# Half-size weight transfers, and matrix-vector work between half units, in a float32 decoder trunk

## The chip, the cores and the metric

The kernel runs on one core of a Trainium2 chip. The metric is the device time of one execution in microseconds, median of several runs. The engines: PE (TensorE) multiplies matrices, ACT (ScalarE) and DVE (VectorE) do elementwise work, POOL (GpSimd) does little here, and SP (SyncE) issues nearly all transfers from device memory. Each engine works through its own instructions in order and waits on semaphores for the others.

## The reference

A trunk of two layers on one sequence of 256 tokens, width 2048. All weights are float32. Each of the four sub-layers is normalised and modulated by vectors made from a conditioning vector `c`:

```python
cond = jax.nn.silu(c)
for l in range(DEPTH):                                   # DEPTH = 2
    mod = cond @ ada_w[l] + ada_b[l]                     # ada_w[l]: 2048 x 12288
    sh1, sc1, g1, sh2, sc2, g2 = jnp.split(mod, 6, axis=-1)
    h = modulate(rmsnorm(x, norm_mix_g[l]), sh1, sc1)    # h * (1 + sc) + sh
    y = mixer_ab(h, ...) if l % 2 == 0 else mixer_c(h, ...)
    x = x + g1 * y
    h = modulate(rmsnorm(x, norm_ffn_g[l]), sh2, sc2)
    x = x + g2 * swiglu(h, ffn_w1[l], ffn_w3[l], ffn_w2[l])   # width 5632
return rmsnorm(x, final_g)
```

`mixer_ab` has one input projection 2048 x 4096 (`ab_w_in`), a causal convolution of width 31 (`a_conv_w`) with a layer norm on one half, spatial gating on the other, and an output projection 2048 x 2048. `mixer_c` is a pooling mixer with four 512 x 512 matrices.

## The kernel before

All weights, 537 MB, stream once from device memory through a ring of buffers named `raw`, the pool `rawp`: six buffers of 1 MB (`RAW = 6`). SP issues each load as soon as a buffer of the ring is free again.

**Products.** The tokens lie in two blocks of 128 (`NB = 2`, index b). Activations are kept transposed and in two parts, `ah` and `al` (the float32 value rounded to PE's fast format, and the rest); q = 0 to 3 numbers groups of 512 input channels, and `act[q][b]` holds the two parts of one group and block. A *unit* (`unit`, `load`) is a 512 x 512 tile of weights. It is split in two halves of 256 rows: ACT casts the half to `hi` (L165) and DVE subtracts to get `lo` (L166), in rings of four (`HL = 4`). Then PE does 12 products a half: for both blocks and two k-tiles hi·ah (L206) and hi·al (L207), and lo·ah (L212) behind them. `block` does the same for several units.

**Matrix-vector work.** The vectors of `mod` come as `cond @ ada_w`, generators that make one step at each `next`. `mod_cols` (L365 on) makes 512 columns of one vector: four steps, each with one load of 512 x 512 and four matmuls with a 32-column broadcast of `cond` (L382, tile `ps_ada`); the fourth also copies the sum to `rows` on ACT (L399); the rest, run by `close`, adds the four strips with four small matmuls (`ps_col`, L412), and DVE adds the bias and writes columns of `gs` (scale) or `sh` (shift). `mod` (L308) makes a whole vector as a row, with wide loads of 128 x 2048 (L304). `weighed` (L343, L354) does the sums on DVE instead. Such work is called a *matvec* below, as one matmul of it.

**The stage of `started`.** It runs the first three column groups of layer 0's input projection while the scale and shift columns of the next group are still being made, since `h` of group q needs only group q's columns. For each q it first writes the instructions that scale the activations of q (`scaled`: `h` at L506, half of it on ACT and half on DVE, then the cast to `ah`, L495), then units u = 0, 1, 2. A matvec generator pair (scale, shift) for q+1 goes beside them: after u0 the scale's four steps, after u1 the shift's four steps; each is closed in the middle of the next unit. The third unit's sums are called `mt`. Before the stage, SP loads the scale matrix for q = 0 (4 units), then x (two blocks of 1 MB, L984), then the shift matrix; ACT squares x (L465, `junk`), x is normalised and transposed (`tp`, L486), copied to `xT`. Small parameters are loaded on ACT's queue at the start, among them `a_conv_w` (31 rows, L621) into tile `prm`. PE transposes the parameters (`tp`, L634 and L639) into `wcT` and `cw` behind q = 0, in `params`.

**Order of the work.** The program is written as these loops; a scheduler then places instructions of independent work in each engine's order by their expected readiness. DMA completions use eight semaphores in rotation over both queues (SP and ACT) in the order of the program, and a transfer waits until the one before it on its semaphore is done.

Of the kernel before, what the change touches and what calls it, by code (L numbers as in the profile page):

```python
# [8 lines left out]
F32 = mybir.dt.float32  # L9
F32R = mybir.dt.float32r  # L10
AF = mybir.ActivationFunctionType
ALU = mybir.AluOpType
PSUM = bass.MemoryType.PSUM

P = 128
D = 2048
KT = D // P
# [3 lines left out]
DH = D // 2  # L21
# [2 lines left out]
PADA = CW - 1  # L24
PADC = 16
EPS = 1e-6
RAW, HL = 6, 4
RATES = 1.56, 0.71, 0.5, 1.0, 1.0
PE2 = False
PE3 = True  # L30
# [6 lines left out]
class Trunk:  # L37
# [119 lines left out]
        return t  # L157


    def split(self, raw, h):  # L160
        nc = self.nc
        hi = self.hip.tile([P, 2, 512], F32R, name="hi", tag="hi")
        lo = self.lop.tile([P, 2, 512], F32R, name="lo", tag="lo")
        part = raw[:, 2 * h : 2 * h + 2, :]
        nc.scalar.copy(hi, part)  # L165
        nc.vector.tensor_tensor(lo, part, hi.bitcast(F32), op=ALU.subtract)  # L166
        for _ in range(FILL):
            self.filler()
        return hi, lo
# [8 lines left out]
                self.fill.pop(0)  # L178

    def load(self, w, row0, col0):  # L180
        raw = self.rawp.tile([P, 4, 512], F32, name="raw", tag="raw")
        self.nc.sync.dma_start(
            out=raw,
            in_=w[row0 : row0 + 512, col0 : col0 + 512].rearrange("(k p) n -> p k n", p=P),
        )
        return raw

    def unit(self, w, row0, col0, act, ps, first, last, mid=None):


        raw = self.load(w, row0, col0)
        for h in range(2):
            if h == 1 and mid is not None:
                mid()
            hi, lo = self.split(raw, h)
            for b in range(NB):
                self.products(hi, lo, h, act, b, ps, first)
            for b in range(NB):
                self.products_lo(hi, lo, h, act, b, ps, last)
        self.after_unit()  # L200
# [15 lines left out]
    def block(self, cells, hooks={}):  # L216


        parts = []
        for w, row0, col0, *_ in cells:  # L220
            raw = self.load(w, row0, col0)
            parts.append([self.split(raw, h) for h in range(2)])
        for b in range(NB):
            for u, (_, _, _, act, ps, first, last) in enumerate(cells):
                for h in range(2):
                    for f in hooks.get((b, 2 * u + h), ()):
                        f()
                    hi, lo = parts[u][h]
                    self.products(hi, lo, h, act, b, ps, first)
                    self.products_lo(hi, lo, h, act, b, ps, last)  # L230
        for _ in cells:
            self.after_unit()
# [62 lines left out]
    def mod(self, l, v, on_pe, then):  # L295


        nc = self.nc
        w = self.i["ada_w"][l]
        if on_pe:  # L300
            ps = self.adap.tile([P, 512], F32, name="ps_ada", tag="ada")
            for k in range(KT):
                raw = self.rawp.tile([P, 4, 512], F32, name="raw", tag="raw")
                nc.sync.dma_start(  # L304
                    out=raw.rearrange("p a n -> p (a n)"), in_=w[k * P : (k + 1) * P, v * D : (v + 1) * D]
                )
                for j in range(4):
                    nc.tensor.matmul(  # L308
                        ps[32 * j : 32 * j + 32, :], self.cond[:, k : k + 1].to_broadcast([P, 32]),
                        raw[:, j, :], start=k == 0, stop=k == KT - 1, skip_group_check=True,  # L310
                    )
                if k < KT - 1:
                    yield
        else:
            ps = None
            for hh in range(2):
                acc = self.accp.tile([P, DH], F32, name="acc", tag="acc")
                for _ in self.weighed(acc, l, v * D + DH * hh):
                    yield
                if ps is None:  # L320
                    ps = self.adap.tile([P, 512], F32, name="ps_ada", tag="ada")
                for j in range(2):
                    o = 32 * (2 * hh + j)
                    nc.tensor.matmul(
                        ps[o : o + 32, :], self.ones[:, :32], acc[:, 512 * j : 512 * j + 512],
                        start=True, stop=True, skip_group_check=True,
                    )
                if hh == 0:
                    yield
        rows = self.wk.tile([P, 512], F32, name="rows", tag="rows", bufs=1)  # L330
        nc.vector.tensor_tensor(  # L331
            rows, ps, self.load_rows(self.i["ada_b"][l, v * D : (v + 1) * D]), op=ALU.add
        )
        then(rows)
        yield

    def weighed(self, acc, l, col0):

        nc = self.nc
        for u in range(KT // 2):  # L340
            raw = self.rawp.tile([P, 4, 512], F32, name="raw", tag="raw")
            r2 = raw.rearrange("p (k a) n -> p k (a n)", k=2)
            nc.sync.dma_start(  # L343
                out=r2,
                in_=self.i["ada_w"][l, 2 * u * P : 2 * (u + 1) * P, col0 : col0 + DH].rearrange(
                    "(k p) n -> p k n", p=P
                ),
            )
            for j in range(2):
                k = 2 * u + j  # L350
                if k == 0:
                    nc.vector.tensor_scalar(acc, r2[:, j, :], self.cond[:, 0:1], None, op0=ALU.mult)
                else:
                    nc.vector.scalar_tensor_tensor(  # L354
                        acc, r2[:, j, :], self.cond[:, k : k + 1], acc, op0=ALU.mult, op1=ALU.add
                    )
            if u < KT // 2 - 1:
                yield
# [10 lines left out]
    def mod_cols(self, l, v, q, on_pe, dst, gname=None):  # L369


        nc = self.nc
        if on_pe:
            acc = self.adap.tile([P, 512], F32, name="ps_ada", tag="ada")
        else:
            acc = self.accp.tile([P, 2, 512], F32, name="accq", tag="acc")
        for u in range(4):
            raw = self.load(self.i["ada_w"][l], 512 * u, v * D + 512 * q)
            for j in range(4):
                k = 4 * u + j  # L380
                if on_pe:
                    nc.tensor.matmul(  # L382
                        acc[32 * j : 32 * j + 32, :], self.cond[:, k : k + 1].to_broadcast([P, 32]), raw[:, j, :],
                        start=u == 0, stop=u == 3, skip_group_check=True,
                    )
                elif k < 2:
                    nc.vector.tensor_scalar(
                        acc[:, k, :], raw[:, j, :], self.cond[:, k : k + 1], None, op0=ALU.mult
                    )
                else:  # L390
                    nc.vector.scalar_tensor_tensor(
                        acc[:, k % 2, :], raw[:, j, :], self.cond[:, k : k + 1], acc[:, k % 2, :],
                        op0=ALU.mult, op1=ALU.add,
                    )
            if u < 3:
                yield
        if on_pe:
            rows = self.wk.tile([P, 512], F32, name="rows", tag="rows", bufs=1)
            nc.scalar.copy(rows, acc)  # L399
            parts = [(rows, self.pick)]  # L400
        else:
            parts = [(acc[:, n, :], self.ones[:, :1]) for n in range(2)]
        yield
        self.put_cols(parts, 4, l, v, 4 * q, dst, gname)
        yield
# [125 lines left out]
    def close(self, g):  # L531
        if g in self.bg:
            for _ in g:
                pass
            self.bg.remove(g)

    def started(self, e, w_cols, rate, then=None):

        self.rate = 0.0
        ps = [self.banks(), self.banks()]
        ps.append([self.tpp.tile([P, 512], F32, name=f"mt{b}", tag="tp") for b in range(NB)])
        for g in e.parts[0]:
            self.close(g)
        for q in range(4):
            e.act[q] = [self.scaled(e.act[q][b], q, b, e.gs, e.sh) for b in range(NB)]
            nxt = e.parts[q + 1] if q < 3 else ()
            for u, (w, col0) in enumerate(w_cols):
                mid = (lambda g=nxt[u - 1]: self.close(g)) if nxt and u > 0 else None  # L550
                self.unit(w, 512 * q, col0, e.act[q], ps[u], q == 0, q == 3, mid)
                if nxt and u < 2:
                    self.advance(nxt[u], 4)
            if q == 0 and then is not None:
                then()
        self.rate = rate
        return ps
# [514 lines left out]
```

## Time and profile before

| | |
|---|---|
| median of 3 runs | 2023.05 us (2021.81, 2026.48, 2023.05) |
| profiled execution | 2021.9 us, span of the records 2020.2 us |
| mean granted PE clock | 0.991 |
| PE busy | 1968.7 us, 97% |
| DVE, ACT busy | 1342.7 us, 839.1 us |
| moved from device memory | 536.68 MB, mean 267 GB/s |

The records of the span are one execution. A line such as `PE mt L206 <- ACT hi L165` names a wait: PE's line 206, for tile `mt`, waited for ACT's line 165, tile `hi`. A matmul of float32 data such as a matvec makes two records, so x16 matvecs of the program are x32 in a timeline. The clock that is granted to PE is 1.00 or 0.50.

### The profile page before, as it was taken

What the parts mean: (1) busy time and instruction counts of PE and PEld (TensorE: products, weight loads), DVE (VectorE), ACT (ScalarE), POOL (GpSimd) and SP (SyncE); (2) the same over time, 40 slices, a digit from 0 to 9 for tenths busy, and PEclk for the clock granted to TensorE, in tenths of its full rate; (3) what the DMA queues carried; (4) which work ended last, traced back from release to release, by engine and by line L of the source; (5) the groups of instructions that cost most, each with busy time, mean ns of one, the idle gap of its engine ahead of it and who ended that gap; (6) DMA issues with size and microseconds to landing.
All of it is one profiled execution on the core that took longest, in us unless ns stands there. A gap on an engine that the chain in (4) does not pass through costs nothing.

```text
span 2020.2 us, 23411 instructions
## 1 busy us (share of the span) xinstructions
PE 1968.7 (97%) x9136; PEld 1541.6 (76%) x9136; DVE 1342.7 (66%) x1596; ACT 839.1 (42%) x1029; POOL 34.1 (2%) x91
## 2 busy tenths in 40 slices
PE   5989999999999999999999999999999999999998
PEld 2557676767887888887878887788788888888886
DVE  2337998656777887777877788777555444554455
ACT  3233243445444343443344436544433444334443
POOL 0000000000000000000120000000000000000000
PEclk9989999999999999999999999999999999999999
DMA  9897988786888898888988877788655555555551
GB/s 348 301 371 283 353 300 308 264 300 219 294 316 301 323 336 316 302 304 316 343 293 305 297 274 267 292 296 309 226 187 188 188 188 188 187 188 190 190 189 57
DMA packets 240160, 540.30 MB, mean 267 GB/s; under 512 B 8394, under 2 KB 9722, under 8 KB 237617
## 3 DMA queue, kind: packets, MB, share of 16 engines
q1 hardware_dynamic: 238296, 536.95, 74.8%
q10 hardware_dynamic: 1752, 1.86, 0.3%
q8 instruction: 71, 1.16, 0.2%
q14 instruction: 41, 0.33, 0.0%
HBM read 536.68 MB, written 2.10 MB: 267 GB/s over the span
## 4 chain that ended last, share of the span: by engine, by line
PE 96%; DVE 1%; ACT 1%; DMA 1%; issue 0%; POOL 0%; ACTq 0%; POOLq 0%; SPq 0%
PE mm L206 28%; PE mm L207 27%; PE mm L212 27%; PE ps_ada L382 3%; PE ps_col L412 1%; PE mt L206 1%; PE mt L207 1%; PE mt L212 1%; PE tp L589 1%; PE ps_ada L308 1%; DMA st_b<-in_ada_b_dram 1%; PE tp L486 1%; PE tp L836 1%; DMA raw<-in_ada_w_dram 0%; PE ps_bc L436 0%
## 5 line engine op out<-in xcount | busy, mean ns | idle before, releaser
L166 DVE TENSOR_TENSOR lo<-raw,hi 128x1024 fp32r<-128x1024 f32 x632 | 767.6, 1222 | 434.8 <-ACT hi L165 426.7
L165 ACT CAST hi<-raw 128x1024 fp32r<-128x1024 f32 x632 | 661.5, 1054 | 894.8 <-PE mm L207 825.4
L206 PE MATMUL mm<-hi,ah 128*128 128x512 f32 x1568 | 618.1, 394 | 5.4 <-ACT hi L165 3.4
L207 PE MATMUL mm<-hi,al 128*128 128x512 f32 x1568 | 612.8, 391 | 0.0
L212 PE MATMUL mm<-lo,ah 128*128 128x512 f32 x1568 | 421.9, 390 | 0.0
L206 PEld LDWEIGHTS mm<-hi,ah 128*128 128x128 f32 x1568 | 295.4, 188 | 83.4 <-ACT hi L165 10.2
L207 PEld LDWEIGHTS mm<-hi,al 128*128 128x128 f32 x1568 | 295.5, 188 | 61.3 <-DVE lo L166 1.2
L212 PEld LDWEIGHTS mm<-lo,ah 128*128 128x128 f32 x1568 | 294.8, 188 | 61.7
L206 PE MATMUL mm<-hi,hh 128*128 128x512 f32 x704 | 279.9, 398 | 0.0
L207 PE MATMUL mm<-hi,hl 128*128 128x512 f32 x704 | 277.9, 395 | 0.0
L354 DVE SCALAR_TENSOR_TENSOR acc<-raw,cond,acc 128x1024 f32<-128x1024 f32 x180 | 230.4, 1280 | 19.6 <-DMA raw<-in_ada_w_dram 18.1
L212 PE MATMUL mm<-lo,hh 128*128 128x512 f32 x704 | 194.7, 395 | 0.0
L206 PEld LDWEIGHTS mm<-hi,hh 128*128 128x128 f32 x704 | 132.3, 188 | 34.3 <-ACT hi L165 1.7
L212 PEld LDWEIGHTS mm<-lo,hh 128*128 128x128 f32 x704 | 132.2, 188 | 32.0
L207 PEld LDWEIGHTS mm<-hi,hl 128*128 128x128 f32 x704 | 132.3, 188 | 30.9
L674 DVE SCALAR_TENSOR_TENSOR co<-aT,cw,co 128x256 f32<-128x256 f32 x240 | 97.9, 477 | 0.0
L382 PE MATMUL ps_ada<-raw,cond 128*32 128x512 f32 x576 | 86.8, 627 | 0.8 <-DVE rows L331 0.8
L597 DVE TENSOR_TENSOR gy<-mm,gate 128x512 f32<-128x512 f32 x72 | 47.1, 685 | 39.9 <-PE mm L212 39.7
L206 PE MATMUL mm<-hi,mh 128*128 128x512 f32 x160 | 64.5, 404 | 0.9 <-ACT mh L495 0.9
L207 PE MATMUL mm<-hi,ml 128*128 128x512 f32 x160 | 63.0, 395 | 0.0
L399 ACT COPY rows<-ps_ada 128x512 f32<-128x512 f32 x18 | 10.5, 585 | 109.7 <-PE ps_ada L382 109.6
L598 DVE TENSOR_TENSOR x<-x,gy 128x512 f32<-128x512 f32 x72 | 47.2, 685 | 0.2
(167 smaller groups left out, 992.7 us busy)
## 6 DMA issues: line engine op xcount, KB each, us to landing
raw<-in_ffn_w_dram SPq DMA_DIRECT2D x264, 1024.0 KB, 5.2
raw<-in_ada_w_dram SPq DMA_DIRECT2D x192, 1024.0 KB, 6.9
raw<-in_ab_w_in_dram SPq DMA_DIRECT2D x32, 1024.0 KB, 7.5
raw<-in_ab_w_out_dram SPq DMA_DIRECT2D x16, 1024.0 KB, 4.9
raw<-in_pool_w_dram SPq DMA_DIRECT2D x4, 1024.0 KB, 5.5
x<-in_x_dram SPq DMA_DIRECT2D x2, 1024.0 KB, 14.2
gate<-in_final_g_dram SPq DMA_DIRECT2D x1, 1024.0 KB
out_dram<-x SPq DMA_DIRECT2D x2, 512.0 KB, 3.7
```

The costliest lines, as they stand in the source:

```text
L165: nc.scalar.copy(hi, part)
L166: nc.vector.tensor_tensor(lo, part, hi.bitcast(F32), op=ALU.subtract)
L206: nc.tensor.matmul(ps[b], act[b][0][:, kk, :], hi[:, k, :], start=first and kk == 0, stop=False)
L207: nc.tensor.matmul(ps[b], act[b][1][:, kk, :], hi[:, k, :], start=False, stop=False)
L212: self.nc.tensor.matmul(ps[b], act[b][0][:, kk, :], lo[:, k, :], start=False, stop=last and kk == 3)
L308: nc.tensor.matmul(ps[32 * j : 32 * j + 32, :], self.cond[:, k : k + 1].to_broadcast([P, 32]), raw[:, j, :], start=k == 0, stop=k == KT - ...
L354: nc.vector.scalar_tensor_tensor(acc, r2[:, j, :], self.cond[:, k : k + 1], acc, op0=ALU.mult, op1=ALU.add)
L382: nc.tensor.matmul(acc[32 * j : 32 * j + 32, :], self.cond[:, k : k + 1].to_broadcast([P, 32]), raw[:, j, :], start=u == 0, stop=u == 3, s ...
L412: nc.tensor.matmul(ps[:, a : a + 1], src[:, P * a : P * a + P], one, start=u == 0, stop=u == len(parts) - 1,)
L597: nc.vector.tensor_tensor(t, ps, g[:, 512 * q : 512 * q + 512], op=ALU.mult)
L598: nc.vector.tensor_tensor(xs, xs, t, op=ALU.add)
L674: nc.vector.scalar_tensor_tensor(co[:, k, :], src, cw[:, k, j : j + 1], co[:, k, :], op0=ALU.mult, op1=ALU.add,)
```

## The change

Every load of weights and matvec matrices is halved: the ring has twelve buffers of 512 KB, `load` brings 256 rows x 512 columns, and the new `load_wide` 128 rows x 1024 columns. `unit` and `block` load two halves and split each. In `started` the two generators of q+1 are advanced in six slots, in the middle and at the end of each unit, by `between`: the scale takes two steps in the middle of u0 and two after u0, is closed in the middle of u1, where the shift takes two steps; the shift takes two more after u1, and is closed in the middle of u2.

```diff
-RAW, HL = 6, 4
+RAW, HL = 12, 4
...
-    def split(self, raw, h):
+    def split(self, raw):
...
-        part = raw[:, 2 * h : 2 * h + 2, :]
-        nc.scalar.copy(hi, part)
-        nc.vector.tensor_tensor(lo, part, hi.bitcast(F32), op=ALU.subtract)
+        nc.scalar.copy(hi, raw)
+        nc.vector.tensor_tensor(lo, raw, hi.bitcast(F32), op=ALU.subtract)
...
     def load(self, w, row0, col0):
-        raw = self.rawp.tile([P, 4, 512], F32, name="raw", tag="raw")
+        raw = self.rawp.tile([P, 2, 512], F32, name="raw", tag="raw")
...
-            in_=w[row0 : row0 + 512, col0 : col0 + 512].rearrange("(k p) n -> p k n", p=P),
+            in_=w[row0 : row0 + 256, col0 : col0 + 512].rearrange("(k p) n -> p k n", p=P),
...
+    def load_wide(self, w, row0, col0):
+        raw = self.rawp.tile([P, 2, 512], F32, name="raw", tag="raw")
+        wide = raw.rearrange("p a n -> p (a n)")
+        self.nc.sync.dma_start(out=wide, in_=w[row0 : row0 + P, col0 : col0 + DH])
+        return raw, wide
...
     def unit(self, w, row0, col0, act, ps, first, last, mid=None):
-        raw = self.load(w, row0, col0)
+        raws = [self.load(w, row0 + 256 * h, col0) for h in range(2)]
         for h in range(2):
             if h == 1 and mid is not None:
                 mid()
-            hi, lo = self.split(raw, h)
+            hi, lo = self.split(raws[h])
...
     def weighed(self, acc, l, col0):
...
-            for j in range(2):
-                k = 2 * u + j
+            for k in (2 * u, 2 * u + 1):
+                raw = self.load_wide(self.i["ada_w"][l], k * P, col0)[1]
...
     def mod_cols(self, l, v, q, on_pe, dst, gname=None):
-            raw = self.load(self.i["ada_w"][l], 512 * u, v * D + 512 * q)
+            raws = [self.load(self.i["ada_w"][l], 512 * u + 256 * h, v * D + 512 * q) for h in range(2)]
...
+    def between(self, gens, slot):
+
+        if gens and slot in (2, 4):
+            self.close(gens[slot // 2 - 1])
+        if gens and slot < 4:
+            self.advance(gens[slot // 2], 2)
+
     def started(self, e, w_cols, rate, then=None):
...
-                mid = (lambda g=nxt[u - 1]: self.close(g)) if nxt and u > 0 else None
-                self.unit(w, 512 * q, col0, e.act[q], ps[u], q == 0, q == 3, mid)
-                if nxt and u < 2:
-                    self.advance(nxt[u], 4)
+                self.unit(
+                    w, 512 * q, col0, e.act[q], ps[u], q == 0, q == 3, lambda: self.between(nxt, 2 * u)
+                )
+                self.between(nxt, 2 * u + 1)
```

The rows below are each engine's instructions in the order in which it works through them, before and after (the line numbers of the two versions differ by a few).

PE, q = 0, from the last products of u1 to the first of u2 (`mm_314` and `mm_315` are the sums of u1 for the two blocks, `mt_316` that of u2). Before:

```order
L212 MATMUL mm_314<-lo,ah_349 128x512 x2
L212 MATMUL mm_315<-lo,ah_358 128x512 x2
L382 MATMUL ps_ada<-raw,cond 32x512 x16
L412 MATMUL ps_col<-pick,rows 128x1 x4
L634 MATMUL tp<-ident,prm 128x128 x4
L639 MATMUL tp<-ident,prm 128x31 x4
L634 MATMUL tp<-ident,prm 128x128 x4
L206 MATMUL mt_316<-hi,ah_349 128x512
```

After the change (`mm_324`, `mm_325` and `mt_326` are these sums):

```order
L214 MATMUL mm_325<-hi,al_375 128x512
L378 MATMUL ps_ada<-raw,cond 32x512 x2
L219 MATMUL mm_324<-lo,ah_365 128x512 x2
L219 MATMUL mm_325<-lo,ah_374 128x512
L378 MATMUL ps_ada<-raw,cond 32x512 x2
L219 MATMUL mm_325<-lo,ah_374 128x512
L378 MATMUL ps_ada<-raw,cond 32x512 x8
L408 MATMUL ps_col<-pick,rows 128x1 x4
L637 MATMUL tp<-ident,prm 128x128 x4
L642 MATMUL tp<-ident,prm 128x31 x4
L213 MATMUL mt_326<-hi,ah_365 128x512
```

The one group of sixteen shift matvecs has become five, of 2, 2, 2, 2 and 8 (the first two stand earlier, in the second half of u1); one set of four 128x128 transposes no longer stands ahead of u2. The same happens in q = 1 and q = 2, without the transposes; in the whole stage 7 groups become 25.

ACT, at the start of u2 in q = 1 (`h_769`, `h_778` and `ah_774` belong to the activations of q = 2, blocks 0 and 1; the two `hi` to u2 of q = 1). Before:

```order
L399 COPY rows<-ps_ada 128x512 [waits PE_49,Activation_49]
L506 ACTIVATE h_769<-xT_252,sh_141,gs_140 128x128 [waits DVE_49]
L506 ACTIVATE h_769<-xT_252,sh_141,gs_140 128x128
L506 ACTIVATE h_778<-xT_294,sh_141,gs_140 128x128
L495 CAST ah_774<-h_769 128x512 [waits DVE_49,Activation_49]
L165 CAST hi<-raw 128x1024 [waits DMAHW4_49]
L165 CAST hi<-raw 128x1024
```

After the change (the tiles are now `h_829`, `ah_834` and `h_838`):

```order
L395 COPY rows<-ps_ada 128x512 [waits PE_49,Activation_49]
L502 ACTIVATE h_829<-xT_262,sh_141,gs_140 128x128 [waits DVE_49]
L502 ACTIVATE h_829<-xT_262,sh_141,gs_140 128x128
L164 CAST hi<-raw 128x1024 [waits DMAHW1_49]
L491 CAST ah_834<-h_829 128x512 [waits DVE_49,Activation_49]
L164 CAST hi<-raw 128x1024 [waits DMAHW2_49]
L502 ACTIVATE h_838<-xT_304,sh_141,gs_140 128x128 x2
```

The first `hi` of u2 now stands ahead of `ah` and of block 1's `h`, and each `hi` waits for a transfer of its own.

SP, at the start of the program. `DMAHW3_49` is the completion semaphore on which the load of `a_conv_w` stands before the change, `DMAHW4_49` the one on which it stands after it. Before:

```order
L182 DMA raw<-in_ada_w_dram 128x4x512
L182 DMA raw<-in_ada_w_dram 128x4x512 [waits DMAHW0_49]
L182 DMA raw<-in_ada_w_dram 128x4x512 [waits DMAHW4_49]
L182 DMA raw<-in_ada_w_dram 128x4x512 [waits DMAHW7_49]
L182 DMA raw<-in_ada_w_dram 128x4x512 [waits DMAHW1_49]
L984 DMA x_190<-in_x_dram 128x2048 [waits DMAHW2_49]
L984 DMA x_201<-in_x_dram 128x2048 [waits DMAHW3_49]
```

After the change:

```order
L182 DMA raw<-in_ada_w_dram 128x2x512 [waits DMAHW5_49]
L182 DMA raw<-in_ada_w_dram 128x2x512 [waits DMAHW6_49]
L182 DMA raw<-in_ada_w_dram 128x2x512 [waits DMAHW7_49]
L182 DMA raw<-in_ada_w_dram 128x2x512 [waits DMAHW2_49]
L182 DMA raw<-in_ada_w_dram 128x2x512 [waits DMAHW4_49]
L182 DMA raw<-in_ada_w_dram 128x2x512 [waits DMAHW5_49]
L182 DMA raw<-in_ada_w_dram 128x2x512 [waits DMAHW6_49]
L987 DMA x_200<-in_x_dram 128x2048 [waits DMAHW7_49]
L987 DMA x_211<-in_x_dram 128x2048 [waits DMAHW0_49]
```

Before, only the second block of x stood behind the load of `a_conv_w`; after the change the eighth half of `ada_w` does, with two more halves and both blocks of x behind it on the queue.

More of the change, by code (lines that the diff above doesn't have):

```diff
@@ L220, in block @@
         for w, row0, col0, *_ in cells:
-            raw = self.load(w, row0, col0)
-            parts.append([self.split(raw, h) for h in range(2)])
+            raws = [self.load(w, row0 + 256 * h, col0) for h in range(2)]
+            parts.append([self.split(r) for r in raws])
         for b in range(NB):
@@ L302, in mod @@
             for k in range(KT):
[L303 to L306, printed above, removed]
+                raws = [self.load_wide(w, k * P, v * D + DH * h)[0] for h in range(2)]
                 for j in range(4):
@@ L309, in mod @@
                         ps[32 * j : 32 * j + 32, :], self.cond[:, k : k + 1].to_broadcast([P, 32]),
-                        raw[:, j, :], start=k == 0, stop=k == KT - 1, skip_group_check=True,
+                        raws[j // 2][:, j % 2, :], start=k == 0, stop=k == KT - 1, skip_group_check=True,
                     )
@@ L340, in weighed @@
         for u in range(KT // 2):
[L341 to L348, printed above, removed]
-            for j in range(2):
-                k = 2 * u + j
+            for k in (2 * u, 2 * u + 1):
+                raw = self.load_wide(self.i["ada_w"][l], k * P, col0)[1]
                 if k == 0:
-                    nc.vector.tensor_scalar(acc, r2[:, j, :], self.cond[:, 0:1], None, op0=ALU.mult)
+                    nc.vector.tensor_scalar(acc, raw, self.cond[:, 0:1], None, op0=ALU.mult)
                 else:
                     nc.vector.scalar_tensor_tensor(
-                        acc, r2[:, j, :], self.cond[:, k : k + 1], acc, op0=ALU.mult, op1=ALU.add
+                        acc, raw, self.cond[:, k : k + 1], acc, op0=ALU.mult, op1=ALU.add
                     )
@@ L382, in mod_cols @@
                     nc.tensor.matmul(
-                        acc[32 * j : 32 * j + 32, :], self.cond[:, k : k + 1].to_broadcast([P, 32]), raw[:, j, :],
+                        acc[32 * j : 32 * j + 32, :], self.cond[:, k : k + 1].to_broadcast([P, 32]), raws[j // 2][:, j % 2, :],
                         start=u == 0, stop=u == 3, skip_group_check=True,
@@ L387, in mod_cols @@
                     nc.vector.tensor_scalar(
-                        acc[:, k, :], raw[:, j, :], self.cond[:, k : k + 1], None, op0=ALU.mult
+                        acc[:, k, :], raws[j // 2][:, j % 2, :], self.cond[:, k : k + 1], None, op0=ALU.mult
                     )
@@ L391, in mod_cols @@
                     nc.vector.scalar_tensor_tensor(
-                        acc[:, k % 2, :], raw[:, j, :], self.cond[:, k : k + 1], acc[:, k % 2, :],
+                        acc[:, k % 2, :], raws[j // 2][:, j % 2, :], self.cond[:, k : k + 1], acc[:, k % 2, :],
                         op0=ALU.mult, op1=ALU.add,
```

## The prediction

> **What bounds the kernel now.** I read the page's busy times first, then tables of windows for the stages, then the waits of PE (TensorE) inside one stage, and last short stretches of the timeline. A windows row gives start:end, its length, then busy us and instructions of PE, weight load, DVE, ACT and POOL, the granted PE clock, the DMA share and GB/s; a wait row gives total us, times and longest.
>
> ```profile
> PE 1968.7 (97%) x9136; PEld 1541.6 (76%) x9136; DVE 1342.7 (66%) x1596; ACT 839.1 (42%) x1029; POOL 34.1 (2%) x91
> 48.00:152.00 104.00, 91.17 (x483) 59.48 (x484) 36.27 (x55) 35.28 (x51) 0.00 (x0) 0.92 0.88 336
> 152.00:440.00 288.00, 287.10 (x1452) 199.46 (x1452) 227.63 (x398) 108.00 (x149) 3.66 (x4) 1.00 0.84 304
> 466.00:2010.00 1544.00, 1542.37 (x6968) 1256.22 (x6967) 1049.40 (x1075) 659.89 (x760) 22.98 (x66) 1.00 0.72 254
> PE mt L206 <- ACT hi L165: 6.0, 2, 3.0
> PE ps_col L412 <- ACT rows L399: 4.7, 6, 1.1
> PE mm L206 <- ACT hi L165: 3.4, 1, 3.4
> PE tp L639 <- DVE wcT L635: 0.8, 1, 0.8
> PE mm L206 <- ACT ah L495: 2.0, 1, 2.0
> 90.00:92.00 2.00, 2.00 (x13) 1.36 (x14) 0.00 (x0) 0.58 (x1) 0.00 (x0) 1.00 0.00 0
> 120.00:122.00 2.00, 2.00 (x11) 1.65 (x10) 0.00 (x0) 0.00 (x0) 0.00 (x0) 1.00 1.05 408
> 124.00:126.00 2.00, 2.00 (x17) 0.95 (x19) 0.00 (x0) 0.00 (x0) 0.00 (x0) 1.00 0.00 0
> SPq L182 <- DVE lo L166: 977.9, 232, 14.3
> ```
>
> PE bounds the kernel. From 152 us on it is busy 287.10 of 288 and 1542.37 of 1544 us, so nothing that only moves transfers can gain there. The stage of `started`, 48 to 152 us, is different: 91 of 104 us busy at a mean clock of 0.92. The first four wait rows, all of that window, are for ACT and DVE work on data that has already landed; none is for a transfer. The fifth is at the start of the first feed-forward part, near 458 us. The DMA engines reach 408 GB/s and then stand still at 90 and at 124 us while PE is fully busy: the ring is full, and SP waits for splits (978 us of waiting for `lo`).
>
> **The change, part by part.** The profiled execution took 2021.9 us; the median of the runs is 2023.05, 1.15 more. I sum against the first and then add the 1.15.
>
> *The ring and the halves.* Twelve buffers of 512 KB hold the same 6 MB, and the bytes stand in the same order on SP's queue. The number of splits, products and DVE matvec steps stays, with the same tiles. What is added is 508 DMA issues and their semaphores on SP. An issue took 0.41 us (the row of `cs`, below), so 208 us more in all; SP's 978 us of waiting for `lo` cover it. If that cover were gone, the loads would come late, which is a rival below. A half buffer comes free after its own `lo`, so loads may start a little earlier; that gain goes into a DMA idle time that PE never waits for. I take 0; below by the ends of the two DMA rivals.
>
> *The matvecs between half units.* In the stage of `started` PE's matvecs stood in 7 groups and stand in 25 after the change, by the order of instructions: 18 more interruptions of the products. The price of one is read where the kernel already does this (start us, us, what):
>
> ```profile
> 179.73 1.07 PE L212 MATMUL mm<-lo,ah 128*128 128x512 f32 x4
> 180.73 1.92 PE L308 MATMUL ps_ada<-raw,cond 128*32 128x512 f32 x16
> 182.59 0.50 PE L206 MATMUL mm<-hi,ah 128*128 128x512 f32 x1
> 257.95 1.07 PE L212 MATMUL mm<-lo,ah 128*128 128x512 f32 x4
> 258.95 1.06 PE L382 MATMUL ps_ada<-raw,cond 128*32 128x512 f32 x8
> 259.94 0.50 PE L206 MATMUL mm<-hi,ah 128*128 128x512 f32 x1
> 67.87 3.64 PE L382 MATMUL ps_ada<-raw,cond 128*32 128x512 f32 x32
> ```
>
> Four products at the stride of 0.227 us (1.07 less the last one's tail) take 0.91. From the first of the four to the next product there are 2.86 us at 179.73 and 1.99 at 257.95, so 1.95 and 1.08 belong to 8 and to 4 matvecs (a matvec is two records). The difference, 0.87 for 4, is 0.217 each; what is left, 0.21 to 0.23, is fixed for each group. A group of 16 by this is 3.66 us, against the 3.64 shown. So 18 x 0.23 = **+4.1 us**, all on PE's path. No group of two is seen in this trace: the ends are 0 (its fixed part overlaps the product behind it) and twice, 8.2. I take the middle value, since three group sizes agree on it.
>
> *The start of u2.* After the last group of q, PE does `ps_col` and then waits for `hi`.
>
> ```profile
> 107.31 1.05 PE L412 MATMUL ps_col<-pick,rows 128*128 128x1 f32 x8 [0.76 <-ACT rows L399]
> 111.36 0.80 PE L206 MATMUL mt<-hi,ah 128*128 128x512 f32 x1 [3.00 <-ACT hi L165]
> 108.59 1.26 ACT L506 ACTIVATE h<-xT,sh,gs 128x128 f32<-128x128 f32 x3 [1.34 <-DVE sh L418]
> 109.76 0.60 ACT L495 CAST ah<-h 128x512 fp32r<-128x512 f32 x1
> 110.27 1.99 ACT L165 CAST hi<-raw 128x1024 fp32r<-128x1024 f32 x2
> 72.30:75.72 3.42, 1.99 (x16) 1.69 (x16) 1.88 (x6) 2.08 (x6) 0.00 (x0) 1.00 1.05 408
> 106.44:109.85 3.41, 1.16 (x12) 0.97 (x8) 1.27 (x5) 1.84 (x5) 0.00 (x0) 1.00 1.05 410
> 109.85:113.26 3.41, 1.90 (x5) 1.53 (x6) 2.61 (x3) 3.38 (x7) 0.00 (x0) 0.50 1.05 407
> 113.26:116.68 3.42, 3.42 (x10) 2.68 (x9) 3.38 (x4) 1.93 (x3) 0.00 (x0) 0.50 1.06 411
> 137.16:140.57 3.41, 2.65 (x27) 0.77 (x19) 0.00 (x0) 0.58 (x1) 0.00 (x0) 1.00 1.05 409
> 140.57:143.98 3.41, 0.80 (x8) 0.72 (x7) 1.85 (x6) 2.37 (x5) 0.00 (x0) 1.00 1.05 408
> 143.98:147.40 3.42, 3.02 (x7) 2.44 (x8) 3.17 (x5) 3.39 (x6) 0.00 (x0) 0.50 1.05 408
> ```
>
> u2 works on the old activations, but ACT prepares part of the next ones first. The new order puts the first `hi` before the third `h` and the `ah` cast: (109.76 - 108.59)/3 + (110.27 - 109.76) = 0.39 + 0.51 = 0.90 us earlier, in q1 and in q2. PE's gap goes from 3.0 to 2.1. The `h` and `ah` behind it are due only when u2 ends, some five us later, so nobody waits for them.
>
> The clock must be counted too. In the rows it halves in stretches of 3.41 us, and always right behind a stretch in which PE was busy 1.99 us or less; behind 2.65 it stayed full. I slid the pattern (0.76 idle, 1.05 `ps_col`, the gap) over such a grid in small steps, with a half stretch behind each one under 2.4 us busy. The loss of one place, idle and half clock together, averages 5.8 us for a gap of 3.0 (4.9 to 6.7) and 4.75 for 2.1 (4.0 to 5.7). The two places of this profile lost 6.4 and 5.3 by the same count, just the mean. So 2 x -1.05 = **-2.1 us**; ends -3.7 (both at 4.0) and -0.3 (both at 5.7).
>
> The Trainium skill, "TensorE: Matmul & The Clock Gate", Part 1, says that the clock falls to half after at least one idle window of about 3.4 us, and its rule for kernels asks for no PE gap over about 3 us. The 3.41 us raster agrees. The trigger does not: the window at 106.44 had 1.16 us of work and the one at 72.30 had 1.99, and each was followed by half clock. By the rule read strictly the new gap of 2.1 would leave the clock alone, which is the second rival.
>
> In q0 the same place holds transposes of parameters as well. Four of them move behind the first products of u2, and with them part of a wait of 0.8 for `wcT`: **-0.4 us**. Ends: 0, and -1.9 if the stretch at 72.30 then has over 2.65 us of work and the 1.5 us lost to the half clock behind it go too.
>
> *The start.* Completion semaphores of transfers are used in rotation, and the new count shifts them.
>
> ```profile
> 0.80 0.41 SPq L74 DMA_DIRECT2D cs<-in_c_dram  x1
> SPq L984 <- DMA prm<-in_a_conv_w_dram: 8.0, 1, 8.0
> 12.65 8.73 SPq L984 DMA_DIRECT2D x<-in_x_dram  x2
> x<-in_x_dram SPq DMA_DIRECT2D x2, 1024.0 KB, 14.2
> raw<-in_ab_w_out_dram SPq DMA_DIRECT2D x16, 1024.0 KB, 4.9
> 28.04 0.63 ACT L465 ACTIVATE junk<-x 128x512 bf16<-128x512 f32 x1
> ```
>
> Now SP stands 8.0 us behind `conv_w`, from 13.0 to 21.0, with 5 MB of matrix and x0 already issued; x0 lands at 12.65 + 14.2 = 26.9, and ACT squares it at 28.0. In the new order the eighth half is what waits for `conv_w`, and behind it on SP's queue stand two more halves, x0 and x1. From 21.0: 1.5 MB and x0 at 408 GB/s (1 MB in 2.57 us) take 6.4, plus 2.3 from issue to first data (4.9 - 2.57), so x0 lands at 29.7 and the squares begin 1.6 late. The chain from there over the transposes to u0 has PE and ACT work only: **+1.6 us**. Ends: -1.0 if `conv_w` itself lands early because less stands before it, +3 if SP waits for more of the small transfers.
>
> *The rest.* The start of the first feed-forward part shuffles a few instructions around its wait of 2.0 for `ah`; I take 0, ends -2 and +2. The 4 KB rows of `load_wide` instead of 8 KB ones lie in a stretch where PE is 100% busy: 0.
>
> Sum: 4.1 - 2.1 - 0.4 + 1.6 = +3.2. The profiled execution would be 2025.1, the median **2026.2 us**, 0.16% up. About 0.2%, 4 us, is what a measurement can tell from no change.
>
> **The rivals.**
> 1. *The idle DMA was the loss.* 12% of the stage's 104 us (share 0.88) are DMA idle; finer buffers would close it and bring the stage 12.5 us forward: 2013.7. Against it: no wait of PE names a transfer.
> 2. *The clock stays full behind a gap of 2.1.* Then a u2 place loses 0.76 + 2.1 = 2.87 instead of 4.75, twice: -3.8, giving 2022.4. For it: the largest busy value followed by half clock in these rows is 1.99. Against it: in any raster one of the two stretches around the gap loses over 1.4 us of its 3.41, which leaves it about 2.0.
> 3. *A group of two costs double.* It has products on both sides and little to fill its own pipeline. At 0.46 for each of 18: 2026.2 + 4.1 = 2030.3, slower. It decides from 0.28 on, where the sum passes 4 us.
> 4. *Halves leave a pause on the queue.* The stage moves 35 MB, so 33 more transfers; its 12.5 us of DMA idle absorb 0.38 us each. At 0.5, 33 x 0.5 - 12.5 = +4: 2030.2. The full 408 GB/s over many transfers speak against a pause now. The Trainium skill, "DMA: Bandwidth & Descriptors", asks for transfers of at least 1 MiB and gives about 2.0 us fixed for each; as an estimate, 508 x 2.0 = 1016 us more if nothing overlapped. The trace already has 0.5 MB in every 1.3 us with many in the queue, so that does not apply here as it stands.
> 5. *The groups cost nothing*, because the products' weight loads fill them: 2026.2 - 4.1 = 2022.1.
>
> **How the numbers follow.** My forecast 0.46; rival 1 0.06, 2 0.14, 3 0.18, 4 0.05, 5 0.11. The first is faster by over 0.2%; 2 and 5 sit within it but with their terms' ends reach below, so faster 0.10. Rivals 3 and 4 are mostly slower, and of my own case a quarter, whose ends reach past +4: slower 0.34. The rest, 0.56, is within 0.2%. Between rival 2 with the q0 stretch saved as well (2022.4 - 1.9 = 2020.5) and rival 3 with a start 1 us worse (2031.3) lie all but rival 1 and tails: 2020.5 to 2031.3.
>
> **What would show it.** The matvecs of the stage in groups of x4 and x16 records, and the next product about 0.23 us late behind each; PE's two waits for `hi` before `mt` near 2.1; half-clock stretches near u2, one each; SP's wait for `conv_w` on a load of `ada_w` and not on x, and the first squares near 29.7 us; PE from 152 us on as busy as before. I would be wrong if a PE wait for a transfer appears, if half-clock stretches come or go elsewhere, or if a group of two costs clearly more or less than 0.23.

## The result, and the profile after

The changed kernel takes 2035.53 us, median of 4 runs (2032.14 to 2036.31), against 2023.39 for the kernel before (2021.81 to 2026.48): a ratio of 1.0058, 95% interval 1.0046 to 1.0071. It is 0.6% slower, outside the predicted range of 2020.5 to 2031.3. The profiled executions differ by 13.9 us (spans 2034.1 and 2020.2).

To see where, I divided both executions at the same products: the first, the 217th, the 1081st and the 1201st hi or lo product of PE. The rows of windows are first those of the kernel before, then those of the changed one (start:end, length, busy us and instructions of PE, weight load, DVE, ACT, POOL, clock, DMA share, GB/s):

```profile
48.59:151.37 102.78, 90.54 (x481) 58.92 (x481) 35.99 (x54) 34.34 (x50) 0.00 (x0) 0.92 0.88 335
151.37:426.39 275.02, 274.12 (x1390) 189.54 (x1388) 220.52 (x388) 102.31 (x141) 3.66 (x4) 1.00 0.84 303
426.39:469.81 43.42, 40.41 (x205) 30.25 (x201) 29.03 (x52) 27.78 (x48) 2.01 (x2) 0.92 0.73 265
469.81:2020.20 1550.39, 1539.24 (x6953) 1253.28 (x6951) 1048.63 (x1076) 657.98 (x756) 23.53 (x67) 1.00 0.72 254
```

```profile
48.28:163.39 115.11, 105.23 (x480) 59.48 (x481) 35.89 (x54) 34.02 (x50) 0.00 (x0) 0.91 0.91 322
163.39:445.16 281.77, 280.03 (x1389) 192.47 (x1387) 221.00 (x388) 102.55 (x141) 3.67 (x4) 0.99 0.84 292
445.16:485.12 39.96, 37.99 (x204) 28.21 (x201) 27.21 (x49) 25.82 (x45) 1.10 (x2) 1.00 0.80 278
485.12:2034.10 1548.98, 1538.11 (x6953) 1252.84 (x6951) 1050.28 (x1079) 659.27 (x759) 23.54 (x67) 1.00 0.76 254
```

The stage of `started` is 12.3 us longer (115.11 against 102.78). The next piece is 6.8 longer, the start of the first feed-forward part 3.5 shorter, the long rest 1.4 shorter, the start 0.3 shorter. In the stage PE does the same instructions and is busy 14.7 us longer: the time did not go into waits. The waits of PE there shrank where the prediction said so, and none is for a transfer:

```profile
PE mt L213 <- ACT hi L164: 4.2, 2, 2.1
PE ps_col L408 <- ACT rows L395: 4.5, 6, 0.8
PE mm L213 <- ACT hi L164: 3.4, 1, 3.4
PE tp L642 <- DVE wcT L638: 0.8, 1, 0.8
```

The matvecs hold the lost time. In the same two windows of the stage, the tile `ps_ada` alone (first before, then after) keeps PE busy 10.5 us longer, of the 12.3:

```profile
48.59:151.37 102.78, 23.26 (x192) 5.79 (x192) 0.00 (x0) 3.51 (x6) 0.92 0.88 335
48.28:163.39 115.11, 33.81 (x192) 5.78 (x192) 0.00 (x0) 3.52 (x6) 0.91 0.91 322
```

Over the whole execution the same 576 records of the single-column-group matvecs keep PE busy 98.1 us, where they kept it 86.8 (groups by line, first before, then after: busy us, mean ns of one):

```profile
L382 PE MATMUL ps_ada<-raw,cond 128*32 128x512 f32 x576 | 86.8, 627 | 0.8 <-DVE rows L331 0.8
```

```profile
L378 PE MATMUL ps_ada<-raw,cond 128*32 128x512 f32 x576 | 98.1, 629 | 0.8 <-DVE rows L335 0.8
```

The timeline of PE in u1 of q = 0 of the changed kernel shows how (two records are one matvec):

```profile
65.60 1.07 PE L219 MATMUL mm<-lo,ah 128*128 128x512 f32 x4
66.60 1.05 PE L378 MATMUL ps_ada<-raw,cond 128*32 128x512 f32 x4
67.58 0.50 PE L213 MATMUL mm<-hi,ah 128*128 128x512 f32 x1
68.01 1.05 PE L378 MATMUL ps_ada<-raw,cond 128*32 128x512 f32 x4
68.99 0.50 PE L214 MATMUL mm<-hi,al 128*128 128x512 f32 x1
...
74.06 1.92 PE L378 MATMUL ps_ada<-raw,cond 128*32 128x512 f32 x16
```

A group of two matvecs (x4) takes 1.05 us, and in the kernel before a group of four (x8, at 258.95) took 1.06. Eight (x16) take 1.92. So the time does not go by matvecs but by sets of four: about 0.86 us for each set begun, and some 0.2 on top. The four matvecs of a step write to four strips of 32 output columns each, and the strips run side by side; two alone leave half of PE's columns idle for the same 0.86 us. The rows of the groups show the overlap: 576 records of 627 ns in 86.8 us of busy time are 4.2 at once on average. A half transfer brings only two strips' data, and the scheduler places these two as soon as it expects them there.

### The profile page after: what moved, and what is told of

Read it like the earlier page. It is cut to its first block, busy times and chain, and to the rows that moved or that the text cites. A ratio compares the mean times of both kernels' runs of the same rounds, so it can differ in the third digit from the quotient of the medians.

```text
span 2034.1 us, 24618 instructions
## 1 busy us (share of the span) xinstructions
PE 1985.5 (98%) x9136; PEld 1542.7 (76%) x9136; DVE 1343.1 (66%) x1596; ACT 838.5 (41%) x1029; POOL 33.3 (2%) x91
## 4 chain that ended last, share of the span: by engine, by line
PE 96%; DMA 2%; ACT 1%; DVE 1%; issue 0%; SPq 0%; POOL 0%; POOLq 0%; ACTq 0%
PE mm L213 28%; PE mm L219 27%; PE mm L214 27%; PE ps_ada L378 4%; PE ps_col L408 1%; PE mt L213 1%; PE mt L214 1%; PE mt L219 1%; PE tp L592 1%; PE ps_ada L312 1%; PE tp L482 1%; PE tp L839 1%; DMA prm<-in_a_conv_w_dram 1%; DMA raw<-in_ada_w_dram 1%; DMA x<-in_x_dram 0%; ACT hi L164 0%
## 5 line engine op out<-in xcount | busy, mean ns | idle before, releaser
L378 PE MATMUL ps_ada<-raw,cond 128*32 128x512 f32 x576 | 98.1, 629 | 0.8 <-DVE rows L335 0.8
```

Of the source, the lines that this page charges most:

```text
L378: nc.tensor.matmul(acc[32 * j : 32 * j + 32, :], self.cond[:, k : k + 1].to_broadcast([P, 32]), raws[j // 2][:, j % 2, :], start=u == 0, s ...
```

## Experiments

**e1. Halves, but matvecs after whole units.**

```diff
-                self.unit(w, 512 * q, col0, e.act[q], ps[u], q == 0, q == 3, lambda: self.between(nxt, 2 * u))
-                self.between(nxt, 2 * u + 1)
+                mid = (lambda g=nxt[u - 1]: self.close(g)) if nxt and u > 0 else None
+                self.unit(w, 512 * q, col0, e.act[q], ps[u], q == 0, q == 3, mid)
+                if nxt and u < 2:
+                    self.advance(nxt[u], 4)
```

> The changed kernel with half transfers throughout, but with the matvecs of the stage after whole units as in the kernel before (7 groups of up to 16). Theory P (four 32-column matvecs run side by side on the four column strips of PE in one pass of about 0.86 us, so a group of n pays n/4 passes rounded up, and some 0.3 us for the interruption): the stage is back at the kernel before or 2 us under it, and only 2 more passes and 3 more groups are left behind the stage, +2.6: 2021 to 2026 us. Theory G (each interruption costs 0.65 us, whatever its size): the same. Theory H (the half transfers themselves cost the time): 2032 to 2036, as the changed kernel.

Measured: 2019.57 us, ratio to the kernel before 0.9985 (0.9976 to 0.9994). Theory H falls: with all 508 additional transfers the kernel is not slower than before, and the loss comes with the new places of the matvecs: 0.73% by the two ratios, some 15 us. P and G stand, though 1.4 us below the range that they gave (it was reckoned from 2023; the kernel before takes 2021.81 in these runs). "Not slower" is a net result. The stage is 3.3 us shorter than before the change (99.44 us in the profile), since ACT's new order at u2 stays and PE's two waits there are 2.1 as in the changed kernel; the piece behind the stage is 5.2 longer (280.21), with the two sets and three groups of matvecs more that the expectation names and a half-clock stretch (374.8 to 378.2 us).

**e2. The new places alone, on 1 MB transfers** (the kernel before, with `between` and its call).

> The kernel before with its 1 MB transfers, and only the new places of the matvecs between half units. A 1 MB transfer lets all four strips go together: 18 groups in the stage, 26 passes against 25. P: 1 x 0.86 + 11 x 0.3 = +4.2, about 2027.5 us. G: 11 x 0.65 = +7.2, about 2030.5. H: no change, 2023.

Measured: 2025.77 us, ratio 1.0018 (1.0009 to 1.0027), which is 4.0 us over the 2021.81 of the kernel before in these runs (1.8 to 5.5 by the interval). P said +4.2, G +7.2, H nothing: G falls here, H too. Less the one set, some 0.3 us is left for each of the 11 interruptions (0.1 to 0.4 by the interval; the profile's stage, 5.7 us longer with 0.9 of it through half clock, gives 0.35). The other three quarters of the loss need both parts of the change: halves that let two strips be ready alone, and a place in the products where they are then put.

**e3. The changed kernel with whole fours.** In `mod_cols`, and with the same order of strips in `mod`:

```diff
-            for j in range(4):
+            for j in (2, 3, 0, 1) if on_pe else range(4):
                 k = 4 * u + j
```

> The changed kernel with one thing altered: the four matvecs of a step are written in the order of strips 2, 3, 0, 1, so that the first two wait for the second half transfer and all four stand together. 17 groups and 26 passes in the stage, against 25 and 33 in the changed kernel and 7 and 25 before. P: +0.9 + 10 x 0.3 - 2.1 at the start of u2 = +1.8 to +2.7, about 2025 to 2026.5 us, 9 us under the changed kernel. G: 10 x 0.65 - 2.1 = +4.4, about 2028. H: 2032 to 2036.

Measured: 2012.64 us, ratio 0.9951 (0.9938 to 0.9965): 1.07% under the changed kernel by the two ratios, 22 us, and 9 us under the kernel before. H falls, since the halves stayed. The direction is P's, but the result is 12 us faster than P allowed. What P says of the matvecs holds: in the stage 7 sets and 8 groups fewer than in the changed kernel are 7 x 0.86 + 8 x 0.2 = 7.6 us, and the matvecs' busy time there fell by 8.0, from 33.81 to 25.77 (over the whole execution from 98.1 to 86.2):

```profile
45.78:143.00 97.22, 25.77 (x192) 4.95 (x192) 0.00 (x0) 3.52 (x6) 0.96 1.00 368
```

Most of the rest is in PE's waits in 45 to 170 us and in the clock behind them:

```profile
PE ps_col L408 <- ACT rows L395: 4.6, 6, 0.8
PE mm L213 <- ACT ah L491: 2.1, 1, 2.1
PE mt L219 <- DVE lo L165: 0.6, 2, 0.3
```

The two waits for `hi` before u2 are gone. In this order ACT casts the first `hi` of u2 ahead of all of the next `h`, where the changed kernel did it behind two of them. The timeline of PE and the clock rows of q = 1 show what that is worth:

```profile
103.18 2.78 PE L378 MATMUL ps_ada<-raw,cond 128*32 128x512 f32 x24
106.75 1.05 PE L408 MATMUL ps_col<-pick,rows 128*128 128x1 f32 x8 [0.79 <-ACT rows L395]
107.69 0.50 PE L213 MATMUL mt<-hi,ah 128*128 128x512 f32 x1
```

```profile
106.40:109.80 3.40, 3.05 (x16) 2.37 (x16) 1.93 (x5) 3.00 (x6) 0.00 (x0) 1.00 1.01 348
109.80:113.20 3.40, 3.12 (x15) 2.58 (x15) 3.30 (x5) 3.40 (x7) 0.00 (x0) 1.00 1.05 408
```

u2 starts right behind `ps_col`, and the clock stays full; in the kernel before, half clock set in at both places. Over the stage PE works 6.4 us at half clock, against 19.5 in the changed kernel (in the stretches 48.3 to 51.9, 79.2 to 86.0, 120.2 to 123.6 and 154.3 to 161.1), which is worth about 6.5 us. The stage takes 97.2 us, 17.9 less than in the changed kernel: 8.0 for the matvecs, 6.5 for the clock and 4.0 less idle time make 18.5. The other 3.4 us between the profiled spans (21.3 in all) lie outside the stage, 2.5 of them in the start. So less than half of the gain is the whole sets; more of it comes with the waits and the clock, above all at u2, where the edit changed ACT's order along with the sets.

**e4. Two strips instead of four,** in `mod_cols` of the kernel before, as a direct test of the side-by-side run (`rows` and `pick` are narrowed to the 64 rows used):

```diff
-                        acc[32 * j : 32 * j + 32, :], ...
-                        start=u == 0, stop=u == 3, skip_group_check=True,
+                        acc[32 * (j % 2) : 32 * (j % 2) + 32, :], ...
+                        start=u == 0 and j < 2, stop=u == 3 and j >= 2, skip_group_check=True,
```

> The kernel before, but the matvecs of single column groups use two of PE's four column strips instead of four (each strip sums twice as many steps); the result is the same. Same count of matvecs, transfers and nearly the same groups. P: 72 passes become 144, +72 x 0.86 = +62 us, about 2085 us; a group of 16 takes 7.1 us instead of 3.64. If a matvec simply takes 0.217 us whatever strip it is on (as the prediction reckoned), nothing changes: 2023.

Measured: 2068.92 us (one run). A group of 16 and the group of all of them:

```profile
74.25 7.06 PE L382 MATMUL ps_ada<-raw,cond 128*32 128x512 f32 x32
L382 PE MATMUL ps_ada<-raw,cond 128*32 128x512 f32 x576 | 147.8, 613 | 0.8 <-DVE rows L331 0.8
```

7.06 us against the 7.1 expected, and +61.0 us of busy time against +62. The number of matvecs is the same, so the time goes by sets on different strips; that is shown (613 ns a record, now 2.4 at once). Whether two matvecs of one strip keep each other waiting for the columns or for the sum that both add to, it leaves open. The kernel as a whole rose by 47 us and not by the 62 expected, in part because some of the longer matvecs lie in waits that PE had anyway (the two for `hi` before u2 fell from 6.0 to 2.5 us).

**e5. Whole fours and whole units** (e3 and e1 together).

> The changed kernel with whole fours (strips 2, 3, 0, 1, as in e3) and the matvecs after whole units (as in e1): 6 groups of 16 in the stage, 24 passes; ACT casts the first half of u2 before it scales the next activations, as in e3. Against e1 (2019.57) it differs mainly in that wait of PE before u2. Theory C (the wait of 2.1 us also brings half clock, so that without it a place loses 0.8 us instead of 4.75): 2019.6 - 2 x 3.95 - 4 passes x 0.86 = about 2008. Theory W (only the idle time itself counts, 2 x 2.1): 2019.6 - 4.2 - 3.4 = 2012. Against e3 (2012.64), 11 groups and 2 passes less: 3.3 + 1.7 under it, 2007.6, by the price of groups alone. A theory N, in which e3 was fast for the placing of matvecs between half units: 2019, as e1.

Measured: 2009.06 us, ratio 0.9936 (0.9924 to 0.9949), 10.5 us under e1. C said 2008, W 2012, N 2019. N falls. Between C and W the median favours C, but the runs of either kernel lie 4 to 6 us apart, and the profiles do not settle it. At the two places of u2 the waits of 2.1 us are gone, and one half-clock stretch of 3.4 us is left (133.7 to 137.1 us), against two in e1, three before and three in the changed kernel. That is 4.2 us of waits and about 1.5 of half clock, 5.7 together, where W has 4.2 and C 7.9. The stretch that is left shows that half clock can also come without the wait. Of the 9.1 us between the two profiles only 4.2 lie in the stage (95.25 us against 99.44); 3.6 lie in the piece behind it, where the matvecs take 3.1 us less, and 2.1 in the start.

**e6. The variance's one-column matmuls spread.** The changed kernel has a pair of half-clock stretches at 389.8 to 396.6 us that the kernel before does not have, although PE had been busy all the time. `norm_a` of e5 then reads:

```diff
                         nc.tensor.matmul(
                             ms[:, b : b + 1], sq[:, k, b * P : (b + 1) * P], self.ones[:, :1],
                             start=k == 0, stop=k == HT - 1,
                         )
-                yield
+                        if k % 4 == 3:
+                            for _ in range(4):
+                                yield
```

> e5 with the 16 one-column matmuls of the layer norm's variance (ps_var) spread over three places, 4, 8 and 4, with eight or more products between, instead of 6 and 10 with two products between. Theory C (one-column matmuls count as little activity, so the stretch that holds them is followed by half clock): the two half-clock stretches near 367 to 375 us go, 2 to 3.5 us under e5. If the profile's busy share decides, PE is 100% busy there in both and nothing changes; the half clock there has another cause.

Measured: 2005.94 us, ratio 0.9924 (0.9910 to 0.9937), 3.1 us under e5. The intervals overlap, so the gain itself is likely and not proved. The stretch is gone from the trace, but in the profiles the piece that held it is only 0.8 us shorter, because PE waits 2.0 us for `mh` there, which it did not in e5. The rows before and at the half clock, of the changed kernel and of e5:

```profile
386.36:389.77 3.41, 3.41 (x33) 2.86 (x25) 2.20 (x3) 3.41 (x6) 0.00 (x0) 1.00 0.73 195
389.77:393.18 3.41, 3.41 (x15) 3.22 (x15) 1.14 (x2) 0.79 (x1) 0.90 (x1) 0.51 1.03 387
```

```profile
362.40:365.81 3.41, 3.41 (x28) 3.28 (x28) 0.91 (x3) 1.70 (x2) 0.02 (x1) 1.00 0.92 313
365.81:369.22 3.41, 3.41 (x10) 2.63 (x9) 2.47 (x3) 0.00 (x0) 1.60 (x1) 0.50 1.04 399
...
363.22 2.29 PE L700 MATMUL ps_var<-ones,sq 128*128 128x1 f32 x20
```

PE is 100% busy in both windows ahead of the half clock, but some 70% of that time goes to one-column matmuls. The kernel before also has ten of them in a row, with no half clock behind:

```profile
375.68 2.29 PE L697 MATMUL ps_var<-ones,sq 128*128 128x1 f32 x20
```

By the grid of 3.41 us, counted back from its half clock at 458.01, about 1.9 us of this row fall into one window, against 2.3 to 2.5 in the two others. So where the windows begin may matter as much as the spreading, and one trace of e6 does not tell the two apart. In e6 the last half-clock stretch before the end of the program is 132.6 to 136.0 us. e6 is the fastest of all: 0.8% under the kernel before.

## Why the prediction was wrong

*The matvecs between half units: this step failed.* The term was 18 x 0.23 = +4.1. It took 0.217 us for each matvec plus a fixed 0.23, fitted to groups of 4, 8 and 16. Those are all whole sets of four strips and cannot tell the two prices apart. In sets of four, the 25 groups of the changed kernel begin 33 sets where 25 were begun before: 8 x 0.86 = 6.9, and 18 interruptions at the 0.3 us of e2 add 5.4: 12.3 us, the whole stage's loss (2.4 us less idle time and 2.4 more through half clock cancel). That it comes out so exactly is luck, since the 0.3 is known only between 0.1 and 0.4. The fixed part of a group (0.23) was about right; the price of a pair was wrong. Rival 3 had the sign, but 2030.3 is less than half of the way from the forecast to the result, and its reason was another: a pipeline that a pair does not fill, at 0.46 us fixed. A pair in fact costs 1.07 us (65.60 to 67.58 less four products at 0.227), which is 0.64 over two matvecs at 0.217. The trace of before would have told. In its start stand two groups side by side, of four and of three matvecs:

```profile
38.72 1.06 PE L382 MATMUL ps_ada<-raw,cond 128*32 128x512 f32 x8
40.74 1.06 PE L382 MATMUL ps_ada<-raw,cond 128*32 128x512 f32 x6
```

Three cost what four cost. The Trainium skill, "TensorE: Matmul & The Clock Gate", Part 3, states that matmuls on different 32-wide tiles of the array run concurrently; these rows and e4 agree, and by that rule a pair has the price of four. The prediction did not use it.

*The start of u2.* The 0.90 us came as worked out: two waits of 2.1 instead of 3.0. The clock did not follow the average. By the windows, the first place lost 0.8 + 2.1 and half of the 3.2 us worked at half clock, 4.5 us; the second 0.8 + 2.1 and half of 6.2, 6.0:

```profile
120.16:123.57 3.41, 3.19 (x8) 2.54 (x9) 2.99 (x4) 3.41 (x7) 0.00 (x0) 0.50 1.02 378
123.57:126.98 3.41, 3.41 (x17) 2.81 (x15) 2.94 (x3) 1.42 (x2) 0.00 (x0) 1.00 0.96 345
154.29:157.70 3.41, 2.75 (x7) 2.18 (x8) 2.78 (x3) 3.41 (x6) 0.00 (x0) 0.50 0.95 360
157.70:161.12 3.42, 3.42 (x10) 2.65 (x9) 3.20 (x5) 2.79 (x4) 0.00 (x0) 0.50 0.99 355
```

10.5 against 11.7 before is -1.2 where -2.1 was forecast, inside the ends given. Rival 2 is refuted: gaps of 2.1 us were followed by half clock both times. The rule of the Trainium skill, "TensorE: Matmul & The Clock Gate", Part 1, in its strict reading does not hold here.

*q = 0.* The four transposes moved and the wait for `cw` went, but two half-clock stretches came (79.2 to 86.0 us) where there had been one: about +1 in place of -0.4.

*The start: the order was right, the size wrong.* SP waits for `conv_w` on a load of `ada_w`, but only until 18.8 us, probably since less stood before it (from 16 to 18 us the DMA share is 0.06, where it was 1.08 before); x0 lands 8.7 us later as reckoned, at 27.5, and is squared at once:

```profile
SPq L182 <- DMA prm<-in_a_conv_w_dram: 8.6, 1, 8.6
20.20 7.25 DMA x<-in_x_dram
27.48 0.63 ACT L461 ACTIVATE junk<-x 128x512 bf16<-128x512 f32 x1 [1.77 <-DMA x<-in_x_dram]
```

u0 began at 48.28 instead of 48.59: -0.3 for a forecast of +1.6, within its ends. The assumption that 21.0 stays was the fault.

*The rest, taken as 0,* was +1.9: +6.8 between the stage and the feed-forward part (two sets and three groups of matvecs more, about 2.5, and the half clock behind `ps_var`, 3.4), -3.5 at the feed-forward part, where half clock had stood at 458 us and does not now, and -1.4 behind it. Both moves of half clock recur in e1 and e3 and neither in e2, which speaks for the half transfers as their source; but e4, on 1 MB transfers, has both as well, so this stays open. *The ring and the halves* at 0 hold in e1 as a net result; rivals 1 and 4 have no support, and rival 5 is refuted by e2.

By terms, with the 12.3 worked out above, the runs give +12.3 - 1.2 + 1 - 0.3 + 1.9 = +13.7 us, where +4.1 - 2.1 - 0.4 + 1.6 + 0 = +3.2 was forecast and the profiles differ by 13.9. The term of the matvecs is 8.2 of the difference, 6.9 of it the sets that are not full.

## What to carry to other kernels

Before small matmuls on column strips are moved or their data split, count the sets that run side by side, not the matmuls: a fit over whole sets says nothing of half ones. A smaller transfer need not cost by itself (here, where PE was the limit, it did not), but it changes what the scheduler finds ready and therefore what it pulls apart; keep together what shares a pass by letting the first of it wait for the last piece of data. A PE gap of two microseconds has to be priced with the half clock that may follow, which here cost another 1.6 to 3.1 us.

## What the runs showed of the hardware

Four float32 matmuls of 32 columns on four strips take 0.86 us together, two take the same. The granted clock fell to half behind windows of 3.41 us in which PE was busy 100% of the time but with one-column matmuls for most of it, so the busy share of the profile does not decide alone; what is counted instead, the runs leave open. Behind gaps of 2.1 us it fell both times in the changed kernel, and both times in e1. And the start can differ by some 2 us between two executions: the first product stood at 48.59 us in the profile of before and at 46.62 in e2, whose code is the same up to there.
